# First two projection blocks side by side, state space scalars behind the first mean, second output matrix unsigned on GpSimd

## The chip, the cores and the metric

The kernel runs on one core of one Trainium2 chip. The metric is device time in microseconds (us) of one execution, the median of several runs.

## What is computed

Two layers of a hybrid block on 16 meta tokens and 512 tokens (528 columns), 1024 features. Cut to what the change touches:

```
hn   = rmsnorm(h, norm1_g[l])
proj = hn @ w_in[l]                       # 23 blocks of 128 columns
sq, sk, sv, rq, rk, rv, rg, u = split(proj)
... stick-breaking attention of sq, sk, sv; retention of rq, rk, rv, rg ...
# state space mixer on u, 16 groups of 16 channels, 64 states each
dt = exp(log_dt); mag = exp(lr * dt); ar = mag * cos(li * dt); ai = mag * sin(li * dt)
fr = ((ar - 1) * lr + ai * li) / den;  fi = (ai * lr - (ar - 1) * li) / den
bbr = fr * br - fi * bi;  bbi = fr * bi + fi * br
xr, xi = scan(a, bu)                      # complex linear recurrence
y = xr @ c_re - xi @ c_im                 # the minus sign is what the change moves
y = gelu(y + d * u); so = y * sigmoid(y @ w_glu)
h = h + concat(sb_o, ro, so) @ w_out[l]
h = h + (silu(hn2 @ w_gate[l]) * (hn2 @ w_up[l])) @ w_down[l]
```

## The kernel before, in words

Features lie on the partitions: `h` is eight tiles of 128 x 528. A product of the weights with the features is made in three passes of reduced precision: both operands are split into a high and a low half (`wh` and `wl`, `xh` and `xl`), and `mm3` (line 346) multiplies, for each of the eight feature tiles, high by high, weight high by feature low, and weight low by feature high, each for two halves of 264 columns. One block of 128 output columns is 8 x 3 x 2 = 48 matmuls into two PSUM banks.

A weight block is a `Unit` (line 273): `load` brings it into one of two buffers `wr`, ScalarE casts the high half, and VectorE or GpSimd subtracts it for the low half (the list `WENG` in the plan of line 312 names the engine; the first block has VectorE, the second GpSimd, the third VectorE). `weight()` (line 326) keeps units loading and splitting ahead.

The sum of squares of the first norm is not awaited: the first three blocks (`HOLD`) are multiplied with the unnormed features, `Norm.finish` (line 410) then makes the mean with four matmuls into `nps`, and the evictions on VectorE (`scaled`, line 1073) multiply by its reciprocal root `R`.

At the start `load_h` (line 1027) loads the first feature tile, then the first weight block in four pieces, and the other tiles, with the second weight block behind the fifth tile. `Norm.parts` splits a tile into `xh` (ScalarE) and `xl` (VectorE); the squares follow in a loop of their own (line 1051). Then `first_params` (line 1055) is spawned. It calls `s5_scalars` (line 451), some 70 operations on 16 columns on VectorE, in a chain, and then `s5_params` (line 534).

`s5_params` makes the matrices of the state space mixer of one layer: the input matrices (`ws`, `we`), the output matrices `gg` (line 609, real part `ri` = 0 and imaginary part `ri` = 1, each from two products `gx`), the blocks `bbd` and their products with `gg` into `kps` (line 641), and the phasors. Its argument `engines` is VectorE and GpSimd for the first layer, and GpSimd twice for the second, whose matrices are made during the first layer's feed-forward part. The imaginary output matrix carries a minus sign, so line 629 takes a VectorE instruction with a scalar, whatever `engines` says. `s5_mix` (line 702) waits for these matrices.

The order of the work is written by a planner in the kernel itself: lanes are generators, `spawn` puts one on a list with a due time, and `tick`, called between the matmuls, runs those that are due by a clock of planned engine times (`spend`, line 96). `now[0][1]` is the due time of the lane that runs. Each engine then works through its queue in order; a scheduler of the framework places instructions in the queues by the order of emission and by readiness.

Of the kernel before, what the change touches and what calls it, by code (L numbers as in the profile page):

```python
# [12 lines left out]
ALU = mybir.AluOpType  # L13
# [5 lines left out]
T = NM + S  # L19
# [69 lines left out]
def hybrid_kernel(ctx, tc, A, out, dbg=None):  # L89
# [444 lines left out]
    def s5_params(l, engines, scal, par):  # L534
# [74 lines left out]
        def outputs():  # L609
# [6 lines left out]
            for ri in range(2):  # L616
                mul, add, sub = on(engines[ri])
                pr, pi = powers(0, 5)
                x1, x2 = (gp.tile([P, 640], F32, tag="g", name=nm("gx")) for _ in range(2))
                mul(v4(x1, 5), wide(c_r, 5), pi if ri else pr)  # L620
                mul(v4(x2, 5), wide(c_i, 5), pr if ri else pi)
                yield
                for q in range(2):
                    r = slice(64 * q, 64 * q + 64)
                    for hf in range(2):
                        o = gg[ri, hf][r, :].rearrange("p (m c) -> p m c", c=32)[:, :, 16 * q:16 * q + 16]
                        a, b = (x[r, 320 * hf:320 * hf + 320].rearrange("p (m c) -> p m c", c=16) for x in (x1, x2))
                        if ri:
                            V.scalar_tensor_tensor(out=o, in0=a, scalar=-1.0, in1=b, op0=ALU.mult, op1=ALU.subtract)
                        else:  # L630
                            sub(o, a, b)
                yield
            bbd = [tt("bbd"), tt("bbd")]
            for ri, src in ((0, bbr), (1, bbi)):
                G.memset(bbd[ri][:, :256], 0.0)
                for q in range(2):
                    engines[ri].tensor_copy(
                        out=bbd[ri][64 * q:64 * q + 64, :256].rearrange("p (t c) -> p t c", c=32)[:, :, 16 * q:16 * q + 16],
                        in_=src[64 * q:64 * q + 64])
            yield  # L640
            for hf in range(2):
                yield from banks(1)
# [59 lines left out]
    def s5_mix(l, u, par, ys):  # L702
# [3 lines left out]
        for hf in range(2):  # L706
# [39 lines left out]
            V.tensor_tensor(out=y1, in0=fi, in1=pi, op=ALU.mult)  # L746
            yield
            G.tensor_tensor(out=xr, in0=xr, in1=y1, op=ALU.subtract)
            V.tensor_tensor(out=xi, in0=fr, in1=pi, op=ALU.mult)
            V.tensor_tensor(out=y2, in0=fi, in1=pr, op=ALU.mult)  # L750
            yield
            G.tensor_tensor(out=xi, in0=xi, in1=y2, op=ALU.add)
            yield
            y = tt("ysm")
            for b in range(2):
# [268 lines left out]
        res.append(o)  # L1024


    def load_h(k):
        nc.sync.dma_start(out=h[k], in_=A["h0"][k])
        if k == 0:
            nc.sync.dma_start(out=cols, in_=A["cols"])  # L1030
            u = Unit(*plan[0])
            u.parts = ()
            for i in range(4):
                for _ in u.split(u.load(i, 4)):
                    pass
            units.append(u)
        elif k == 4:
            u = Unit(*plan[1])
            u.load()
            u.parts = u.split()  # L1040
            units.append(u)
            u.use()
            splits[0] = 2

    nrm = Norm(0, 48)
    for k in range(KD):
        load_h(k)
        nrm.parts(k)
    for i in (90, 96):
        G.tensor_scalar(out=cols[:, i:i + 2], in0=cols[:, i:i + 2], scalar1=0.125, scalar2=None, op0=ALU.mult)  # L1050
    for k in range(KD):
        nrm.square(k)
    par = []

    def first_params():
# [3 lines left out]
        yield from s5_params(0, (V, G), scal, par)  # L1059

    scal = []
    spawn(first_params())
    for l in range(LAYERS):
        got = {}
        mix = [None] * 8

        def proj(n, p):
            w = weight()
            ps = open_ps(T)
            mm3(ps, w, nrm.x)  # L1070
            return ps

        def scaled(n, ps):
            t = tt(n)
# [47 lines left out]
        spawn(ret_lane())  # L1122
        held = []
        for i, (n, p) in enumerate(proj_order(l)):
            held.append((n, p, proj(n, p)))
            if i == HOLD[l]:
                nrm.finish()
            if i >= HOLD[l]:
                for n, p, ps in held:
                    spawn(after(n, p, scaled(n, ps)), busy["V"])  # L1130
# [151 lines left out]
```

## Time and profile before

| | |
|---|---|
| median of 3 runs | 1380.3 us (1379.69 to 1380.94) |
| the profiled execution's own time | 1384.1 us |
| its span, first to last instruction | 1382.4 us |
| TensorE (PE) busy | 1352.0 us |
| VectorE (DVE), ScalarE (ACT), GpSimd (POOL) busy | 806.3, 618.1, 514.6 us |
| mean granted clock of TensorE | 0.995 |

The profile comes from one execution. PE is TensorE's matmuls and PEld its weight loads, DVE is VectorE, ACT ScalarE, POOL GpSimd, SPq the queue of SyncE that issues the loads. L121 is a helper through which nearly every instruction goes, so instructions are told apart by the tiles they write and read. A matmul's time in the trace includes its way through the array; how fast they follow one another is read from their starts. Idle time of an engine that is not the bottleneck costs nothing.

### The profile page before, as it was taken

The page shows a single profiled execution, that of the slowest core. Times are in us where ns is not written, and L with a number is a line of the kernel's source. Part 1 is how long each engine was busy: PE and PEld are TensorE (multiplying, and loading weights), DVE is VectorE, ACT ScalarE, POOL GpSimd, SP SyncE. Part 2 cuts the span into 40 slices and gives each one's busy share as a digit, 9 for nine tenths or more (in the row PEclk, how much of TensorE's full clock was granted, in tenths as well). Part 3 has the DMA queues.
Part 4 walks back from the last instruction along what each step waited for, and adds up shares of the span by engine and source line. Part 5 has one row for each costly group of instructions (what it writes and reads, how often), then busy time and mean ns, then how long its engine had stood idle before and what let it go on. Part 6 is the DMA issues. An engine that isn't in the chain of part 4 may idle for free.

```text
span 1382.4 us, 22757 instructions
## 1 busy us (share of the span) xinstructions
PE 1352.0 (98%) x9188; PEld 1241.3 (90%) x9188; DVE 806.3 (58%) x1312; ACT 618.1 (45%) x1002; POOL 514.6 (37%) x624
## 2 busy tenths in 40 slices
PE   6999999999899999999999999999999999999998
PEld 6989999999899999999999998998788888888886
DVE  8874858767456445534567386555585543554453
ACT  5456676555252233312354664874354422332231
POOL 5685648322899112201234534562232210220120
PEclk9999999999999999999999999999999999999999
DMA  4221212323221322322232220123232332233223
GB/s 156 70 74 50 78 46 71 94 77 108 84 78 59 109 92 92 92 92 88 78 110 70 71 93 32 70 59 90 86 105 95 102 93 92 92 96 103 92 79 104
DMA packets 38985, 118.27 MB, mean 86 GB/s; under 512 B 4960, under 2 KB 5472, under 8 KB 38880
## 3 DMA queue, kind: packets, MB, share of 16 engines
q1 hardware_dynamic: 38880, 116.82, 25.9%
q8 instruction: 72, 1.18, 0.3%
q14 instruction: 33, 0.27, 0.1%
HBM read 111.46 MB, written 2.10 MB: 82 GB/s over the span
## 4 chain that ended last, share of the span: by engine, by line
PE 75%; DVE 4%; POOL 3%; issue 1%; ACT 1%; SPq 0%; DMA 0%; DVEq 0%; ACTq 0%
PE pj L133 67%; PE z L133 4%; PE ro L133 1%; PE hps L133 1%; PE av L133 1%; PE yps L133 1%; DVE wl L121 1%; DVE y L121 0%; DVE fr L121 0%; POOL st L121 0%; POOL py L121 0%; PE sc L133 0%; POOL gx L121 0%; POOL bb L121 0%; PE rtp L139 0%
## 5 line engine op out<-in xcount | busy, mean ns | idle before, releaser
L133 PE MATMUL pj<-xh,wh 128*128 128x264 f32 (+1 forms) x1792 | 447.8, 310 | 14.6 <-ACT wh L121 5.3
L133 PE MATMUL pj<-xl,wh 128*128 128x264 f32 (+1 forms) x1792 | 450.5, 311 | 1.6 <-DVE xl L121 1.6
L133 PE MATMUL pj<-xh,wl 128*128 128x264 f32 (+1 forms) x1792 | 447.5, 310 | 1.6 <-DVE wl L121 1.6
L121 ACT CAST wh<-wr 128x1024 fp32r<-128x1024 f32 (+3 forms) x209 | 205.9, 987 | 412.7 <-PE pj L133 378.6
L133 PEld LDWEIGHTS pj<-xh,wh 128*128 128x128 f32 x1792 | 296.8, 190 | 33.1 <-issue 7.4
L133 PEld LDWEIGHTS pj<-xl,wh 128*128 128x128 f32 x1792 | 297.2, 190 | 20.2 <-DVE xl L121 2.4
L133 PEld LDWEIGHTS pj<-xh,wl 128*128 128x128 f32 x1792 | 297.0, 191 | 18.7 <-DVE wl L121 1.8
L121 DVE TENSOR_TENSOR wl<-wr,wh 128x1024 fp32r<-128x1024 f32 (+3 forms) x166 | 249.6, 1505 | 72.4 <-ACT wh L121 72.1
L133 PE MATMUL pj<-hi,wh 128*128 128x264 f32 (+1 forms) x720 | 192.5, 322 | 0.0
L133 PE MATMUL pj<-lo,wh 128*128 128x264 f32 (+1 forms) x720 | 192.4, 321 | 0.0
L133 PE MATMUL pj<-hi,wl 128*128 128x264 f32 (+1 forms) x720 | 191.8, 321 | 0.1
L121 POOL TENSOR_TENSOR up<-ga,up 128x528 f32<-128x528 f32 (+1 forms) x44 | 62.0, 1409 | 344.8 <-DVE up L121 344.7
L121 POOL TENSOR_TENSOR wl<-wr,wh 128x1024 fp32r<-128x1024 f32 (+2 forms) x43 | 96.8, 2252 | 137.3 <-ACT wh L121 117.8
L121 DVE TENSOR_TENSOR h<-h,pj 128x264 f32<-128x264 f32 (+1 forms) x144 | 69.4, 510 | 134.7 <-PE pj L133 134.5
L133 PEld LDWEIGHTS pj<-hi,wl 128*128 128x128 f32 x720 | 119.5, 188 | 11.0 <-DVE wl L121 0.5
L133 PEld LDWEIGHTS pj<-hi,wh 128*128 128x128 f32 x720 | 119.4, 188 | 10.9 <-ACT wh L121 0.6
L133 PEld LDWEIGHTS pj<-lo,wh 128*128 128x128 f32 x720 | 119.4, 188 | 10.5
L121 POOL TENSOR_TENSOR lo<-ga,hi 128x528 fp32r<-128x528 f32 (+1 forms) x44 | 59.0, 1340 | 158.3 <-ACT hi L121 158.2
L121 DVE TENSOR_TENSOR up<-pj,R 128x264 f32<-128x264 f32 (+1 forms) x66 | 32.1, 514 | 95.2 <-PE pj L133 95.2
L121 ACT ACTIVATE si<-si,bias 128x528 f32<-128x528 f32 (+1 forms) x44 | 32.1, 730 | 95.3 <-DVE si L121 95.3
L121 DVE TENSOR_TENSOR ga<-si,up 128x528 f32<-128x528 f32 (+1 forms) x44 | 31.7, 719 | 73.8 <-ACT si L121 58.7
L121 POOL TENSOR_TENSOR lo<-sp,hi 128x432 fp32r<-128x432 f32 (+2 forms) x36 | 46.4, 1301 | 34.4 <-ACT hi L121 34.3
(228 smaller groups left out, 1710.9 us busy)
## 6 DMA issues: line engine op xcount, KB each, us to landing
wr<-in_w_in_dram SPq DMA_DIRECT2D x45, 512.0 KB, 3.4
wr<-in_w_gate_dram SPq DMA_DIRECT2D x44, 512.0 KB, 3.4
wr<-in_w_up_dram SPq DMA_DIRECT2D x44, 512.0 KB, 3.4
wr<-in_w_down_dram SPq DMA_DIRECT2D x32, 512.0 KB, 3.5
wr<-in_w_out_dram SPq DMA_DIRECT2D x16, 384.0 KB, 3.2
wr<-in_w_down_dram SPq DMA_DIRECT2D x16, 384.0 KB, 3.1
rc<-in_rope_dram SPq DMA_DIRECT2D x12, 264.0 KB, 3.7
rs<-in_rope_dram SPq DMA_DIRECT2D x12, 264.0 KB, 3.8
```

What stands on the lines that cost most here:

```text
L121: return f(*a, **k)
L133: nc.tensor.matmul(out, lhsT=lhsT, rhs=rhs, start=start, stop=stop, skip_group_check=more)
```

## The change

The first two blocks are loaded in three pieces each, between the feature tiles, and multiplied tile by tile in turn into four banks. The squares are made between the tiles. `first_params` is spawned after the first mean. The imaginary output matrix loses its sign and is made on the engine that `engines` names; the sign goes into `bbd` and into `xi`. The lane that makes the output matrices gets a due time 2000 ns later before the products with `bbd`.

```diff
--- before.py
+++ after.py
@@ -625,18 +625,16 @@
                     for hf in range(2):
                         o = gg[ri, hf][r, :].rearrange("p (m c) -> p m c", c=32)[:, :, 16 * q:16 * q + 16]
                         a, b = (x[r, 320 * hf:320 * hf + 320].rearrange("p (m c) -> p m c", c=16) for x in (x1, x2))
-                        if ri:
-                            V.scalar_tensor_tensor(out=o, in0=a, scalar=-1.0, in1=b, op0=ALU.mult, op1=ALU.subtract)
-                        else:
-                            sub(o, a, b)
+                        (add if ri else sub)(o, a, b)
                 yield
             bbd = [tt("bbd"), tt("bbd")]
             for ri, src in ((0, bbr), (1, bbi)):
                 G.memset(bbd[ri][:, :256], 0.0)
                 for q in range(2):
-                    engines[ri].tensor_copy(
+                    engines[ri].tensor_scalar(
                         out=bbd[ri][64 * q:64 * q + 64, :256].rearrange("p (t c) -> p t c", c=32)[:, :, 16 * q:16 * q + 16],
-                        in_=src[64 * q:64 * q + 64])
+                        in0=src[64 * q:64 * q + 64], scalar1=-1.0 if ri else 1.0, scalar2=None, op0=ALU.mult)
+            now[0][1] += 2000
             yield
             for hf in range(2):
                 yield from banks(1)
@@ -746,10 +744,10 @@
             V.tensor_tensor(out=y1, in0=fi, in1=pi, op=ALU.mult)
             yield
             G.tensor_tensor(out=xr, in0=xr, in1=y1, op=ALU.subtract)
-            V.tensor_tensor(out=xi, in0=fr, in1=pi, op=ALU.mult)
+            V.scalar_tensor_tensor(out=xi, in0=fr, scalar=-1.0, in1=pi, op0=ALU.mult, op1=ALU.mult)
             V.tensor_tensor(out=y2, in0=fi, in1=pr, op=ALU.mult)
             yield
-            G.tensor_tensor(out=xi, in0=xi, in1=y2, op=ALU.add)
+            G.tensor_tensor(out=xi, in0=xi, in1=y2, op=ALU.subtract)
             yield
             y = tt("ysm")
             for b in range(2):
@@ -1024,32 +1022,33 @@
         res.append(o)
 
 
-    def load_h(k):
+    nrm = Norm(0, 48)
+    units += [Unit(*plan[0]), Unit(*plan[1])]
+    for k in range(KD):
         nc.sync.dma_start(out=h[k], in_=A["h0"][k])
         if k == 0:
             nc.sync.dma_start(out=cols, in_=A["cols"])
-            u = Unit(*plan[0])
-            u.parts = ()
-            for i in range(4):
-                for _ in u.split(u.load(i, 4)):
-                    pass
-            units.append(u)
-        elif k == 4:
-            u = Unit(*plan[1])
-            u.load()
-            u.parts = u.split()
-            units.append(u)
-            u.use()
-            splits[0] = 2
-
-    nrm = Norm(0, 48)
-    for k in range(KD):
-        load_h(k)
-        nrm.parts(k)
+
+        q = []
+        if k < 4:
+            q = [(units[k % 2], k // 2, 4)]
+        elif k < 6:
+            q = [(units[k % 2], 1, 2)]
+        for u, i, pieces in q:
+            c = u.load(i, pieces)
+            nrm.parts(k)
+            for _ in u.split(c):
+                pass
+        if not q:
+            nrm.parts(k)
+        if k:
+            nrm.square(k - 1)
+    nrm.square(KD - 1)
+    for u in units:
+        u.parts = ()
+    splits[0] = 2
     for i in (90, 96):
         G.tensor_scalar(out=cols[:, i:i + 2], in0=cols[:, i:i + 2], scalar1=0.125, scalar2=None, op0=ALU.mult)
-    for k in range(KD):
-        nrm.square(k)
     par = []
 
     def first_params():
@@ -1059,16 +1058,24 @@
         yield from s5_params(0, (V, G), scal, par)
 
     scal = []
-    spawn(first_params())
     for l in range(LAYERS):
         got = {}
         mix = [None] * 8
 
-        def proj(n, p):
-            w = weight()
+        def proj(w):
             ps = open_ps(T)
             mm3(ps, w, nrm.x)
             return ps
+
+        def two_proj():
+
+            ws = [weight(), weight()]
+            pss = [open_ps(T), open_ps(T)]
+            xh, xl = nrm.x
+            for k in range(KD):
+                for ps, w in zip(pss, ws):
+                    mm3(ps, tuple(t[:, k:k + 1, :] for t in w), (xh[k:k + 1], xl[k:k + 1]), first=k == 0, last=k == KD - 1)
+            return pss
 
         def scaled(n, ps):
             t = tt(n)
@@ -1122,9 +1129,16 @@
         spawn(ret_lane())
         held = []
         for i, (n, p) in enumerate(proj_order(l)):
-            held.append((n, p, proj(n, p)))
+            if l == 0 and i < 2:
+                if i == 0:
+                    first = two_proj()
+                held.append((n, p, first[i]))
+            else:
+                held.append((n, p, proj(weight())))
             if i == HOLD[l]:
                 nrm.finish()
+                if l == 0:
+                    spawn(first_params())
             if i >= HOLD[l]:
                 for n, p, ps in held:
                     spawn(after(n, p, scaled(n, ps)), busy["V"])
```

## Rows read from the trace of the kernel before

**Rows 1.** Totals of the page: busy us, share of the span, instructions.
```profile
PE 1352.0 (98%) x9188; PEld 1241.3 (90%) x9188; DVE 806.3 (58%) x1312; ACT 618.1 (45%) x1002; POOL 514.6 (37%) x624
```
**Rows 2.** TensorE's waits over the span: us in total, times, longest.
```profile
PE pj L133 <- DVE xl L121: 1.6, 2, 1.0
PE kps L133 <- POOL bbd L121: 1.5, 1, 1.5
```
**Rows 3.** Timeline, TensorE, 5 to 36 us: start, us, engine, operation, [idle before].
```profile
5.29 0.81 PE L133 MATMUL pj<-xh,wh 128*128 128x264 f32 x2 [5.29 <-ACT wh L121]
...
9.67 0.81 PE L133 MATMUL pj<-xh,wh 128*128 128x264 f32 x2 [2.69 <-ACT xh L121]
...
15.04 0.64 PE L133 MATMUL pj<-xh,wl 128*128 128x264 f32 x2
...
15.48 0.53 PE L133 MATMUL pj<-xh,wh 128*128 128x264 f32 x2
...
25.88 0.41 PE L133 MATMUL pj<-xh,wh 128*128 128x264 f32 x2
...
26.12 0.40 PE L133 MATMUL pj<-xl,wh 128*128 128x264 f32 x2
...
29.63 0.51 PE L133 MATMUL pj<-xh,wl 128*128 128x264 f32 x2 [1.63 <-DVE wl L121]
...
35.10 0.28 PE L133 MATMUL nps<-hi,meanw 128*128 128x264 f32 x1
```
**Rows 4.** Timeline, the other engines, 1 to 16 us.
```profile
1.71 1.85 SPq L284 DMA_DIRECT2D wr<-in_w_in_dram  x4
...
13.29 2.39 POOL L121 TENSOR_TENSOR wl<-wr,wh 128x1024 fp32r<-128x1024 f32 x1 [1.65 <-ACT wh L121]
13.47 2.25 DVE L121 TENSOR_TENSOR s5w<-s5w 128x16 f32<-128x16 f32 x1
```
**Rows 5.** Tile `s5w`, 0 to 45 us: ns min/median/max, first and last start.
```profile
L121 DVE TENSOR_TENSOR s5w<-s5w x19: 161/175/2245, 13.5 to 36.9; 128x16 f32<-128x16 f32 x19
...
L121 DVE TENSOR_TENSOR s5w<-cols,s5w x2: 165/166/168, 5.2 to 5.3; 128x16 f32<-128x16 f32 x2
```
**Rows 6.** Windows: us, busy (instructions) PE, PEld, DVE, ACT, POOL, PEclk, DMA.
```profile
10.00:15.00 5.00, 5.00 (x22) 4.70 (x22) 4.97 (x13) 4.49 (x7) 2.62 (x3) 1.00 0.83 329
...
0.00:35.00 35.00, 23.76 (x144) 22.51 (x145) 28.39 (x96) 17.38 (x28) 19.83 (x44) 0.95 0.45 154
...
60.00:100.00 40.00, 36.58 (x252) 33.73 (x251) 33.73 (x116) 19.30 (x36) 34.35 (x94) 0.91 0.19 67
370.00:375.00 5.00, 2.02 (x13) 2.05 (x14) 4.97 (x9) 0.69 (x2) 5.00 (x10) 0.91 0.00 0
375.00:380.00 5.00, 5.00 (x34) 5.00 (x33) 1.45 (x3) 1.38 (x2) 4.84 (x6) 0.75 0.31 105
```
**Rows 7.** Timeline, 365 to 373 us, GpSimd, VectorE and TensorE.
```profile
366.76 2.64 POOL L121 TENSOR_TENSOR gx<-braw,s5p 128x640 f32<-128x640 f32 x2
...
369.44 2.94 DVE L121 SCALAR_TENSOR_TENSOR gg<-gx,gx 64x320 f32<-64x320 f32 x4 [3.97 <-POOL gx L121]
...
372.98 0.36 PE L133 MATMUL pj<-xh,wh 128*128 128x264 f32 x1 [3.77 <-DVE ga L121]
```
**Rows 8.** Groups, VectorE, 40 to 100 us: busy, mean ns | idle before, releaser.
```profile
L121 DVE TENSOR_TENSOR gx<-braw,s5p 128x640 f32<-128x640 f32 x2 | 3.3, 1682 | 3.9 <-DMA braw<-in_bc_dram 3.9
```
**Rows 9.** Tile `gg`, 0 to 500 us: ns min/median/max, first and last start.
```profile
L121 DVE SCALAR_TENSOR_TENSOR gg<-gx,gx x8: 484/608/1381, 62.5 to 371.9; 64x320 f32<-64x320 f32 x8
...
L121 POOL TENSOR_TENSOR gg<-gx,gx x4: 868/874/879, 360.4 to 363.0; 64x320 f32<-64x320 f32 x4
```
**Rows 10.** Tile `uc`, 0 to 300 us: the state space lane's first instructions.
```profile
L121 ACT COPY uc<-u x16: 418/430/438, 115.5 to 185.9; 32x132 f32<-32x132 f32 x16
```
**Rows 11.** Timeline, VectorE, 276 to 291 us, around the first output projection.
```profile
281.05 0.71 DVE L121 TENSOR_TENSOR lo<-glu,hi 128x528 fp32r<-128x528 f32 x1 [0.29 <-ACT hi L121]
...
289.10 0.76 DVE L121 TENSOR_TENSOR h<-h,pj 128x264 f32<-128x264 f32 x2
```

## The prediction

> **What bounds the kernel now.** I first read the page's totals: TensorE is busy for 1352.0 us, 98% of the span [rows 1]. A change can gain only in the 30 us in which TensorE waits and where its clock is low; work of another engine counts only if a TensorE wait ends with it. So the second view was TensorE's waits, summed by what released them [rows 2]: 1.6 us on the low halves `xl` of the features and 1.5 us on `bbd` are among them; the larger ones stand with their place in the timeline, which came third.
>
> *The start* [rows 3]. TensorE starts at 5.29 us, waits 2.69 us for the second feature tile and later 1.63 us for a low weight half `wl`; the mean of the first norm follows the third block at 35.10 us. Three blocks are 3 x 48 = 144 matmuls. Late in the stretch a pair starts after 0.24 us (25.88, 26.12), 0.12 us each: 17.3 us of work, so 12.5 of these 29.8 us are lost. Part is rate: from 15.04 to 15.48 a pair takes 0.44 us, 0.22 us each, the lower of the two clock levels (1.2 against 2.4 GHz). So it runs from 9.67 on, right after the wait, until about 15.5. The windows view gives a granted clock of 1.00 there [rows 6]; I go by the spacing.
>
> *Why low halves are late.* VectorE's queue holds the scalars of the state space model between the splits, from 5.2 to 37.1 us [rows 5]. They are 16 columns wide with a median of 0.175 us, but the one at 13.47 took 2.25 us, beside GpSimd's weight split of 13.29 to 15.68 [rows 4].
>
> *60 to 100 us.* VectorE (33.7 of 40 us) and GpSimd (34.4) are nearly full, TensorE is busy for 36.6 us and the granted clock is 0.91 [rows 6]: 3.4 us idle, and 40 x 0.09 x 2 = 7.2 us at the lower level, which cost 7.2 x (1 - 0.12 / 0.22) = 3.3 us.
>
> *365 to 380 us*, the first layer's feed-forward part [rows 7]. VectorE's `gg` instruction stands at the head of its queue for 3.97 us until GpSimd has made `gx`; behind it stand the evictions `ga`, which free TensorE's banks. TensorE waits 3.77 us, and then the granted clock is 0.91 and 0.75 in two windows of 5 us [rows 6]: 5 x 0.34 x 2 = 3.4 us at the lower level, 1.5 us lost.
>
> **The change part by part.**
>
> *Two blocks side by side.* Each feature tile gets 12 matmuls instead of 6. The bytes stay; SP issues one load more, at 1.85 / 4 = 0.46 us [rows 4], and the second block's quarters pass ahead of later tiles, so the last tile may land half a microsecond later, when TensorE has a backlog that covers it. SP's load of the third weight waits until the first weight is split and its buffer free, some 4 us later than now; two blocks of 48 x 0.12 = 5.8 us each cover it. In the first 35 us ScalarE is busy for 17.4 us and GpSimd for 19.8 [rows 6]: the same work fits into 29. GpSimd splits the second block's weight in three pieces instead of one of 2.39 us.
> I count the losses that remain: 1.5 us waiting for the second block's first quarter (not shown before; nothing at best, 2.7 us at worst, the wait for a tile that it replaces; I take the middle, as a quarter is half a tile in size); 1.0 us in the first six matmuls (0.6 of rate, 0.4 on their low half); the lower clock for 6 us from about 8 us, as long as before, 27 matmuls x 0.10 = 2.7 us; 1.0 us on low halves. That is 6.2 instead of 12.5: **gain 6** (bounds 3, if both kinds of wait stay, and 9).
>
> *The scalars behind the mean.* They leave VectorE's first stretch (counted above) and come back after the third block, behind that block's evictions. Lines 451 to 532 issue 70 of them: from below 70 x 0.175 = 12 us, from above the 32 us that they take now among the splits. Queued behind them are the evictions of blocks 4 and 5 and the products of the state space matrices. The latter wait for a load that VectorE today awaits for 3.9 us [rows 8], so the first few microseconds are free. But the stretch of 60 to 100 us gets fuller. Its bounds are a gain of 3.4 us (its waits vanish) and a loss of 6.7 (what it costs now, once more); I take **a loss of 1.5**, nearer the row as it stands, since four `gg` instructions (4 x 0.61 us, rows 9) leave VectorE there too.
> The state space lane then starts later. Today it begins at 115.5 us, as its matrices get ready [rows 10], and its last split ends at 281.76, while the output projection that uses it cannot start before the previous part's last pair of evictions at 289.10 [rows 11]: 7.3 us of slack, of which TensorE's 6 us of lead eat most. If the matrices are L later in absolute time, TensorE stands still for L - 1.3 us. I take L = 3, **a loss of 1.7** (bounds 0 and 10).
>
> *The second output matrix on GpSimd.* Four adds at 0.87 us, measured on GpSimd for the same shape [rows 9], 3.5 us a layer, take the place of four VectorE instructions. In layer 2's matrices, made during the first feed-forward part, no VectorE instruction waits for `gx` any more: 3.77 + 1.5 = 5.3 us. GpSimd is full there (5.00 of 5 us, rows 6), so its products for the feed-forward part queue 3.5 us longer, but TensorE needs those only in the down projection; I take off 0.3: **gain 5** (bounds 0 and 5.3). The sign goes into `xi`, where four instructions of VectorE take another form, and into `bbd`, where a multiplication takes the place of a copy: nothing, as TensorE waits nowhere for `xi` (its wait for `bbd` is priced next); without that cover some tenths of a microsecond.
>
> *2000 ns more before the blocks' products.* TensorE waits 1.5 us for `bbd` [rows 2]. The planner now emits these matmuls 2 us later; GpSimd's four adds lie before `bbd`, but the planner prices them itself. **Gain 1.2** (bounds 0 and 1.5).
>
> Sum: 6 + 5 + 1.2 - 1.5 - 1.7 = 9.0 us. The profiled execution took 1384.1 us, so 1375.1; it lies 3.8 us above the median of the runs, 1380.3, which gives 1371.3, rounded **1371 us**.
>
> **A rule against it.** At 13.47 a 0.17 us instruction of VectorE lasted as long as GpSimd's split beside it [rows 4]. The Trainium skill, page "SBUF — State Buffer", section "Who interferes with whom", says that a VectorE instruction with two SBUF inputs and a GpSimd instruction that reads SBUF exclude one another, whichever came first holding the port to its end. The trace agrees (2.25 us against 0.17). By that rule GpSimd's new adds cost VectorE about their own length, which is the third rival. The Trainium skill, page "Perfetto Trace Analysis", section "Optimizing Scalar/DVE Operations", warns likewise that moving work between these two might not help.
>
> **The rivals.**
> 1. *VectorE's crowding takes it back.* The scalars, stretched by GpSimd's instructions, meet evictions at 60 to 100 us, and the 6.7 us lost there double: 5.2 more than I took, 1376. For it: both engines are full there. Against: VectorE idles for 3.9 us just before [rows 8]. Chance 0.18.
> 2. *The state space lane becomes the bound: slower.* Place: the second part of the first output projection. If the scalars take 32 us again, they end at 61 instead of 37 and L is 24; TensorE waits 22.7 us instead of 1.7, 21 more than I took: 1392. It decides from about L = 12 on, where it eats all the gain. Against: VectorE has no splits of feature tiles left between the scalars. Chance 0.08.
> 3. *The port.* GpSimd's adds hold up VectorE's evictions in the feed-forward part for 3.5 us, and TensorE with them: 1374.5. For it: the 2.25 us row. Against: behind an add that lasts 0.87 us there is only a short hold-up, and a block gives TensorE 5.8 us of work. Chance 0.12.
> 4. *More than that.* Nothing lost at 60 to 100 and in the lane, and the start gains 9: 1371.3 - 3 - 3.2, 1365. Chance 0.10.
>
> **How the numbers follow.** My case (1366 to 1376) has 0.52. About 0.2%, 2.8 us, is what a measurement of this kernel can tell from no change: below 1377.5 is faster. Half of rival 1's spread and nearly all of rival 3's lie there, with my case and rival 4: 0.82 faster. The other half of rival 1 and a rest of 3 give 0.10, rival 2 gives 0.08. The range 1364 to 1379 takes in rivals 1, 3 and 4 and leaves out rival 2 and the tails.
>
> **What would show it.** Right, if the first `nps` matmul comes at about 29 us; if no scalar of the state space model stands on VectorE before it; if the wait for `ga` and the lower clock near 370 us are gone, and the wait for `bbd`. Wrong, if TensorE waits at the first output projection's second part, if 60 to 100 us loses far more than 6.7 us, or if the wait near 370 us comes back under another name.

## The result, and the profile after

The changed kernel takes 1392.65 us (median of 4 runs, 1390.1 to 1393.14), the kernel before 1380.62 us beside it: a ratio of 1.0081, 95% interval 1.0066 to 1.0096. It is slower by 12 us, where 9 us of gain were forecast; the range of the prediction ended at 1379. The profiled execution has a span of 1390.7 us, against 1382.4 before. Of all runs below one was slow, 2274.75 us at a mean granted clock of 0.636 (the changed kernel with the early call), and that kernel's figure is the median of its three fast runs.

**Totals.** The page's first part of the kernel after; it answers to [rows 1]:

```profile
PE 1354.9 (97%) x9188; PEld 1245.7 (90%) x9188; DVE 804.5 (58%) x1303; ACT 617.5 (44%) x1003; POOL 512.4 (37%) x634
```

TensorE is busy for 2.9 us more with the same 9188 matmuls, and stands idle for 35.8 us instead of 30.4. VectorE has nine instructions fewer and GpSimd ten more.

**By stretch.** Windows of the kernel after (us, busy time and instructions of PE, PEld, DVE, ACT, POOL, then PEclk, DMA share, GB/s), and under them the same windows of the kernel before from 100 us on:

```profile
0.00:35.00 35.00, 25.85 (x172) 24.98 (x173) 29.76 (x93) 19.60 (x33) 21.61 (x47) 0.95 0.50 169
60.00:100.00 40.00, 35.20 (x274) 33.99 (x273) 31.10 (x99) 19.37 (x34) 32.93 (x85) 1.00 0.17 57
100.00:200.00 100.00, 96.58 (x692) 90.57 (x692) 60.53 (x105) 59.24 (x120) 62.64 (x69) 0.95 0.21 67
200.00:300.00 100.00, 92.94 (x738) 87.58 (x736) 78.88 (x153) 52.06 (x98) 35.95 (x30) 0.97 0.21 63
300.00:400.00 100.00, 94.89 (x769) 93.09 (x769) 59.74 (x90) 43.58 (x63) 52.20 (x51) 0.98 0.29 95
```

```profile
100.00:200.00 100.00, 100.00 (x762) 93.03 (x761) 61.78 (x122) 68.14 (x134) 56.09 (x49) 1.00 0.18 57
200.00:300.00 100.00, 98.70 (x797) 93.95 (x797) 74.91 (x144) 55.85 (x105) 50.80 (x38) 1.00 0.26 78
300.00:400.00 100.00, 96.23 (x781) 96.05 (x780) 61.48 (x92) 44.31 (x63) 57.19 (x77) 0.98 0.28 96
```

Up to 100 us the change gains. The first 35 us hold 172 matmuls instead of 144 [rows 6], and from 60 to 100 us the granted clock is 1.00 where it was 0.91. The loss lies from 100 to 400 us, where little of the change itself stands: TensorE is busy for 284.4 us of these 300 instead of 294.9, and the clock column gives 100 x (0.05 + 0.03 + 0.02) x 2 = 20 us at the lower level instead of 4. A microsecond at the lower level loses 1 - 0.24 / 0.44 = 0.45 us of work, by the pairs of matmuls in [rows 3], so that is 10.5 + 16 x 0.45 = 17.7 us lost. The hundredths of the clock column make this good to a few microseconds.

**Waits.** TensorE's waits over the span of the kernel after, the largest nine; they answer to [rows 2]:

```profile
PE pj L133 <- ACT wh L121: 5.7, 1, 5.7
PE wps L139 <- POOL ws L121: 5.1, 2, 2.7
PE sc L133 <- DVE sc L121: 4.5, 3, 2.8
PE av L133 <- DVE rq L121: 3.4, 1, 3.4
PE pj L133 <- DVE u L121: 3.0, 1, 3.0
PE hps L133 <- ACT hsq L121: 2.6, 3, 1.3
PE pj L133 <- DVE wl L121: 2.2, 1, 2.2
PE pj L133 <- DVE sq L121: 1.8, 1, 1.8
PE ro L133 <- DVE sc L121: 1.5, 1, 1.5
```

The waits for `xl`, for `bbd` and for `ga` are no longer among the large ones. In their place stand `ws` (the input matrices of the second layer), `sc` (retention), `rq` and `u`. By their place in the timeline, the waits of over 1 us between 100 and 400 us are `av` for `rq` at 179.9 us, retention's products `sc` and `ro` at 220.7, 265.9 and 268.5 us (5.7 us together), `hps` at 251.7 us, and `ws` at 394.6 and 398.6 us; `u` and `sq` lie at 77.6 and 83.0 us. At the second part of the first output projection, whose evictions run from 302.3 to 316.8 us, TensorE does not wait, as these windows of the kernel after show:

```profile
290.00:310.00 20.00, 20.00 (x165) 18.30 (x164) 12.25 (x31) 9.92 (x21) 5.49 (x8) 1.00 0.20 55
310.00:330.00 20.00, 20.00 (x167) 20.00 (x166) 17.38 (x34) 11.29 (x17) 6.64 (x4) 1.00 0.38 119
```

**The start.** Timeline of TensorE (it answers to [rows 3]), then the tile `s5w` over the span ([rows 5]), both of the kernel after:

```profile
10.68 0.64 PE L133 MATMUL pj<-xh,wh 128*128 128x264 f32 x2
11.12 0.44 PE L133 MATMUL pj<-xh,wl 128*128 128x264 f32 x2
11.40 0.41 PE L133 MATMUL pj<-xh,wh 128*128 128x264 f32 x2
11.64 0.41 PE L133 MATMUL pj<-xl,wh 128*128 128x264 f32 x2
...
30.06 0.28 PE L133 MATMUL nps<-hi,meanw 128*128 128x264 f32 x1
```

```profile
L121 DVE TENSOR_TENSOR s5w<-s5w x19: 159/166/1327, 9.9 to 38.5; 128x16 f32<-128x16 f32 x19
...
L121 DVE TENSOR_TENSOR s5w<-cols,s5w x2: 168/168/168, 5.2 to 5.3; 128x16 f32<-128x16 f32 x2
```

TensorE no longer waits for the second tile; pairs are 0.44 us apart until 11.12 and 0.24 from 11.40 on, where the change came at about 15.5 before. The first `nps` comes at 30.06 us, 5.0 us earlier. But the scalars stand where they stood: from 5.2 us on, the last one at 38.5 (36.9 before), although the call that issues them now comes behind the third block. Their inputs are ready from the start, and the framework's scheduler places instructions by readiness as well as by the order of emission. Moving the call did not move them.

**The lane.** What did move is the lane behind the scalars. Tile `ws` from 50 to 120 us, first of the kernel before, then of the kernel after (ns min/median/max, first and last start):

```profile
L139 PE MATMUL wps<-ident,ws x16: 272/273/300, 70.1 to 77.2; 128*128 128x128 f32 x16
...
L121 POOL TENSOR_TENSOR ws<-btmp,btmp x4: 922/952/1083, 60.2 to 63.1; 64x256 f32<-64x256 f32 x4
```

```profile
L139 PE MATMUL wps<-ident,ws x16: 270/272/273, 95.4 to 101.1; 128*128 128x128 f32 x16
...
L121 POOL TENSOR_TENSOR ws<-btmp,btmp x4: 733/738/1620, 62.0 to 65.1; 64x256 f32<-64x256 f32 x4
```

The data are 2 us later (65.1 against 63.1), the transposes that read them 25 us later. TensorE waited for nothing there: the transposes stand later in its queue, so the planner placed them later. The state space lane starts at 136.8 us (its first `uc` copy on ScalarE) instead of 115.5 [rows 10].

**Layer 2's matrices.** Timeline of GpSimd and of TensorE and a window, kernel after; they answer to [rows 7] and [rows 6]:

```profile
391.86 7.37 POOL L121 TENSOR_TENSOR ws<-btmp,btmp 64x256 f32<-64x256 f32 x8
...
394.59 1.34 PE L139 MATMUL wps<-ident,ws 128*128 128x128 f32 x8 [2.42 <-POOL ws L121]
...
398.60 1.12 PE L139 MATMUL wps<-ident,ws 128*128 128x128 f32 x4 [2.66 <-POOL ws L121]
```

```profile
396.00:402.00 6.00, 3.40 (x16) 3.41 (x17) 1.24 (x2) 0.93 (x2) 5.78 (x6) 0.57 0.25 87
```

VectorE's wait for `gx` and TensorE's 3.77 us for `ga` are gone. GpSimd, full as before, gives the lost time back 20 us later: TensorE waits 2.42 and 2.66 us for `ws`, and the granted clock is 0.57 behind it.

### The profile page after: what moved, and what is told of

It reads as the page before. It is cut to its first block, busy times and chain, and to the rows that moved or that the text cites. A ratio compares the mean times of both kernels' runs of the same rounds, so it can differ in the third digit from the quotient of the medians.

```text
span 1390.7 us, 22774 instructions
## 1 busy us (share of the span) xinstructions
PE 1354.9 (97%) x9188; PEld 1245.7 (90%) x9188; DVE 804.5 (58%) x1303; ACT 617.5 (44%) x1003; POOL 512.4 (37%) x634
## 4 chain that ended last, share of the span: by engine, by line
PE 84%; DVE 9%; POOL 3%; ACT 1%; issue 1%; DMA 1%; SPq 0%; DVEq 0%
PE pj L133 72%; PE z L133 5%; PE hps L133 1%; PE ro L133 1%; PE av L133 1%; DVE fr L121 1%; DVE s5w L121 1%; DVE ysm L121 1%; DVE fi L121 1%; DVE st L121 1%; DVE y L121 1%; DVE wl L121 1%; POOL ws L121 1%; PE kps L133 1%; POOL gg L121 1%
## 5 line engine op out<-in xcount | busy, mean ns | idle before, releaser
L121 POOL TENSOR_TENSOR up<-ga,up 128x528 f32<-128x528 f32 (+1 forms) x44 | 60.8, 1381 | 344.1 <-DVE up L121 344.1
L121 POOL TENSOR_TENSOR wl<-wr,wh 128x1024 fp32r<-128x1024 f32 (+3 forms) x45 | 97.1, 2158 | 117.5 <-ACT wh L121 107.4
L133 PEld LDWEIGHTS pj<-lo,wh 128*128 128x128 f32 x720 | 119.9, 189 | 10.4
```

Of the source, the lines that this page charges most:

```text
L121: return f(*a, **k)
L133: nc.tensor.matmul(out, lhsT=lhsT, rhs=rhs, start=start, stop=stop, skip_group_check=more)
```

## The experiments

All figures stand against the kernel before on the same chip (medians of 1379.6 to 1381 us). The column "lane starts" is the state space lane's first `uc` copy on ScalarE, "first `ro`" the start of the first retention pair's output products on TensorE, "last split" the end of the split of the state space lane's result, which the output projection's second part needs. These three columns come from one profiled execution of each kernel, which lies up to 8 us from its median.

| kernel | median us | ratio, 95% | lane starts | first `ro` | last split |
|---|---|---|---|---|---|
| before | 1380.6 | | 115.5 | 184.6 | 281.8 |
| after | 1392.65 | 1.0081 (1.0066 to 1.0096) | 136.8 | 223.4 | 298.3 |
| two blocks only | 1377.4 | 0.9979 (0.9970 to 0.9988) | 114.9 | 186.7 | 290.3 |
| late call only | 1399.5 | 1.0139 (1.0117 to 1.0161) | 137.7 | 225.7 | 309.5 |
| unsigned only | 1387.7 | 1.0052 (1.0032 to 1.0072) | 129.3 | 210.5 | 289.9 |
| unsigned, layer 2 | 1380.45 | 1.0003 (0.9993 to 1.0012) | 115.6 | 185.7 | 284.6 |
| unsigned, layer 1 | 1388.3 | 1.0065 (1.0052 to 1.0079) | 129.2 | 210.4 | 290.5 |
| due 1 us later | 1390.6 | 1.0073 (1.0060 to 1.0086) | 125.3 | 244.2 | 296.5 |
| due 2 us earlier | 1399.0 | 1.0129 (1.0108 to 1.0149) | 122.1 | 245.6 | 300.3 |
| one bank kept | 1392.8 | 1.0086 (1.0062 to 1.0109) | 119.9 | 233.6 | 287.0 |

### The parts, one at a time

**The changed kernel with the early call.**

```diff
+    spawn(first_params())
...
-                if l == 0:
-                    spawn(first_params())
```

> The changed kernel with the state space scalars spawned ahead of the projections again, as before; two blocks side by side, unsigned output matrix and the later due time stay. Lane theory (the scalars' new place starts the state space lane 21 us late, and its VectorE work then meets GpSimd's splits at 170 to 270 us, where TensorE lost some 17 us to waits and the lower clock): the lane begins near 115 us again, those losses fall below 4 us, the time is 1374 to 1380. GpSimd theory (the loss comes from the adds that moved to GpSimd): 1388 or more, as in the changed kernel. Start theory (splits of the second block side by side leave the kernel's order worse): also 1388 or more.

1387.9 us, ratio 1.0055 (1.0033 to 1.0077): the early call gives back only 4.7 us. Something else in the change costs as well.

**The late call alone**, in the kernel before:

```diff
-    spawn(first_params())
...
+                if l == 0:
+                    spawn(first_params())
```

> The kernel before with one edit: the scalars are spawned behind the first mean. Lane theory: the lane begins 15 to 25 us later than 115 us, TensorE waits between 170 and 300 us, the time is 1386 to 1395. GpSimd theory: no adds moved, so the time is 1375 to 1383, and the splits of the features are earlier. Start theory: 1375 to 1383 as well.

1399.5 us: 19 us lost by moving one call, with the scalars on VectorE from 5.3 to 36.8 us as before. The transposes of `ws` come at 102.1 us, and its `ws` was ready 33 us earlier (last start 68.2).

**The two blocks side by side alone** (the diff's hunks from line 1024 on, without the move of the call):

> The kernel before with only the first two blocks side by side; scalars early, the signed output matrix on VectorE. Lane theory: the first mean comes 2 to 5 us earlier (33 to 30 us), the lane begins at 110 to 117 us, the time is 1374 to 1379. Start theory: slower than before, 1385 or more. GpSimd theory: 1374 to 1379, like the lane theory.

1377.4 us: faster than both kernels, by 2.9 us against before. The first `nps` comes at 30.1 us as in the kernel after, so 5.0 us of lead become 2.9 at the end.

**The unsigned matrix alone, then layer by layer:**

```diff
-                            V.scalar_tensor_tensor(out=o, in0=a, scalar=-1.0, in1=b, op0=ALU.mult, op1=ALU.subtract)
+                            (engines[1] if l == 1 else V).tensor_tensor(out=o, in0=a, in1=b, op=ALU.add)
...
```

This is the edit for layer 2 alone; layer 1 alone has `l == 0`, and the run with both takes the line of the diff. In all three the signs go into `bbd` and `xi` of both layers, as in the diff.

> The kernel before with only the unsigned output matrix on GpSimd (signs in the blocks and in xi), without the later due time. Lane theory: the 3.8 us wait for the evictions near 370 us goes; GpSimd's queue is 3.5 us longer and the transposes of the input matrices wait for it instead, as in the changed kernel (5 us there), so 1378 to 1383. GpSimd theory: 1386 or more, with the loss in the first layer.

> The kernel before with the unsigned output matrix, made on GpSimd for the second layer's matrices alone; the first layer's stays on VectorE (an add there). Lane theory: the first layer runs as before (the lane begins at 113 to 118 us, the first output projection ends at 322 to 326 us); in the feed-forward part the wait for ga (3.8 us) is replaced by the transposes' waits for GpSimd's ws (some 5 us) with the lower clock behind them, so 1379 to 1383. If the adds in the first layer cost nothing and the feed-forward part alone made the loss of the unsigned matrix, this run would show 1386 to 1389.

> The kernel before with the unsigned output matrix, made on GpSimd for the first layer's matrices alone. Lane theory: the state space lane begins near 129 us as in the run with both, the state space and retention lanes end at 288 to 292 and 309 to 314 us instead of 281.8 and 302.7, TensorE waits at the first output projection, and the time is 1383 to 1388, nearly all of the loss of the unsigned matrix. If the loss sat in the feed-forward part, it would be 1379 to 1382.

Both layers 1387.7 us, layer 2 alone 1380.45, layer 1 alone 1388.3 (1.0065, 1.0052 to 1.0079). So layer 2's part, for which 5 us were forecast, is worth nothing, and layer 1's, priced at nothing, costs 8 to 9. The new signs are in the run with layer 2 alone too, so they are not what costs. TensorE's largest waits with layer 2's part alone:

```profile
PE pj L133 <- ACT wh L121: 5.1, 1, 5.1
PE wps L139 <- POOL ws L121: 4.7, 2, 2.4
PE pj L133 <- DVE wl L121: 4.3, 1, 4.3
```

The wait for `ga` has left the list, 4.7 us for `ws` have come; from 360 to 420 us TensorE is busy for 55.3 us at a clock of 0.94 against 54.8 at 0.97.

The prices of the parts do not add up. Alone they come to 19.1 + 7.3 - 2.9 = 23.5 us of loss; together they make 12.

**Two tries to keep layer 2's gain** beside the two blocks: VectorE's `gg` instructions 6 us later and the products 2 us later, and GpSimd's version with transposes and products 12 us later.

```diff
+                if ri and l:
+                    now[0][1] += 6000
...
```

> Two blocks side by side, scalars early, signed matrix on VectorE; but for the second layer's matrices the lane that makes the output matrices is due 6 us later before VectorE's signed subtraction, and 2 us later before the products with bbd. Lane theory: first layer as in the run with two blocks only (1377.4); the wait for ga near 370 us (3.7 us and 1.5 us of lower clock) and the wait for bbd (1.4 us) go, so 1370 to 1374. If GpSimd's full queue is the bound there and the wait only moves (to ws, as with the adds on GpSimd), 1376 to 1379.

> Two blocks side by side and scalars early as in the run with two blocks only; the unsigned output matrix on GpSimd for the second layer's matrices alone; and for those the transposes of the input matrices and the products with bbd are due 12 us later. Queue theory of the feed-forward part (TensorE meets whatever GpSimd's full queue makes late, and only a later place in TensorE's own order helps): the waits for ga, for ws and for bbd between 360 and 430 us all go, so 1370 to 1374. If another product of GpSimd's queue becomes late instead (up, lo), TensorE waits there and the time is 1376 to 1380.

1379.96 us (1.0006, 0.9996 to 1.0015) and 1380.9 us (0.9998, 0.9986 to 1.0010): both lose the 2.9 us of the two blocks. In the first the wait for `ga` stays at 3.8 us, so, as with the scalars, the due time did not decide the place on VectorE; in the second it is 1.5 us, without profit.

### First theory: a late lane is the price

**The lane held back** by 14 us with its matrices unmoved, and **the matrices 16 us later** with the call unmoved:

```diff
+            if l == 0:
+                now[0][1] = max(now[0][1], busy["PE"]) + 14000
+                yield
```

> The kernel before with nothing moved; the first layer's state space lane is only held back by 14 us in the planner once its matrices are ready. Lane theory: lateness alone is enough; the lane begins at 128 to 132 us, retention and state space end 7 us or more later, TensorE waits before or in the first output projection, and the time is 1384 to 1392. If the loss came from crowded engines (scalars beside evictions, adds on GpSimd) and not from the lane's start, this run would be within 2 us of before, 1379 to 1383.

```diff
         scal.extend(s5_scalars())
+        now[0][1] += 16000
```

> The kernel before, scalars in their place, but the lane that makes the first layer's matrices is due 16 us later in the planner after the scalars. Planner theory (moving the scalars' call did not move them on VectorE, where they start at 5.2 us in every run; it gave the matrices a later due time, and with it TensorE's transposes and products a later place in its order): the transposes come at 90 to 105 us instead of 70, the lane begins at 128 to 140 us, and the time is 1388 to 1400. If the scalars' place itself cost the time, this run is within 3 us of before.

1393.2 us (1.0097, 1.0081 to 1.0112) and 1394.5 us (1.0088, 1.0060 to 1.0116). Lateness as a price would give about this: 13 and 14 us, for 14 and 16. But the runs don't say whether lateness itself is paid for. Lanes ask for PSUM banks with `banks(n)` out of a budget of five (`BANKS`), and wait until n are free at once; a lane that comes later finds others holding them.

**A sixth bank** (`BANKS = 6`), in the kernel after and in the kernel before:

> The changed kernel with the lanes' budget of PSUM banks raised from 5 to 6. Bank theory (a late state space lane is dear because it competes with stick-breaking and retention for the five banks): retention's first pair ends before 235 us instead of 252, its third before 308 instead of 316, and the time falls to 1378 to 1386. If the lateness costs through the planner's order alone, whatever the banks: 1389 to 1395.

> The kernel before with the lanes' budget raised from 5 to 6, the control of the run with six banks. Bank theory: its lanes are not late, so little changes, 1376 to 1384. If six banks take TensorE's own double buffers away, 1385 or more.

1415.6 us (1.0243, 1.0219 to 1.0267) and 1404.5 us (1.0165, 1.0141 to 1.0189): 23 us worse in either. The budget leaves the other banks of the eight to the projections' own double buffering, so this run mixes two things and decides nothing on the order.

### Second theory: the order in which the lanes get the banks

**The due time 1 us later**, nothing else:

```diff
         scal.extend(s5_scalars())
+        now[0][1] += 1000
```

> Edit: the kernel before, with the due time of the lane of the state space matrices 1 us later, behind the scalars, which stay where they are. The race for the banks of the planner's budget: the second input matrix asks for its bank a moment after the attention lanes have taken the free ones, so its transposes on TensorE come 20 us or more later (they start by 76.1 us before), the lane starts at 121 us or later (115.5 before), and the time is at least 4 us above that of the kernel before, 1385 to 1392 us. Lateness of the due time alone: 1 us of due time is worth 1 us or less (16 us of it cost 14 us), nothing moves by more than 2 us, and the time is within 1.5 us of the kernel before.

1390.6 us: one microsecond of due time costs 10. Tile `ws`, 50 to 120 us:

```profile
L139 PE MATMUL wps<-ident,ws x16: 270/272/330, 71.8 to 111.8; 128*128 128x128 f32 x16
...
L121 POOL TENSOR_TENSOR ws<-btmp,btmp x4: 777/869/1196, 57.4 to 62.2; 64x256 f32<-64x256 f32 x4
```

The last transposes go from 77.2 to 111.8 us, 49 us after the last of their data. Lateness as a price of its own cannot do that.

**The late call with the old due time:**

```diff
         scal.extend(s5_scalars())
+        now[0][1] = busy["PE"] + 2700
```

> Edit: the kernel before with the call moved behind the first mean, and the due time of the lane set back to about what it was before the move. Lateness of the due time: the transposes of the input matrices are back at 70 to 77 us, the lane starts at 116 to 118 us, and the time is 1381 to 1383 us. The race for the banks: the order of the requests has changed as well, so the transposes stay at 85 us or later, the lane starts at 125 us or later, and the time is 1388 us or more.

1396.4 us (1.0116, 1.0103 to 1.0130), transposes at 105.2 us, lane at 140.1. Setting the due time back does not bring the lane back.

**The due time 2 us earlier:**

```diff
         scal.extend(s5_scalars())
+        now[0][1] -= 2000
```

> Edit: the kernel before, with the due time of the lane of the state space matrices 2 us earlier, nothing else. If lateness of this lane is the price by itself, an earlier one costs nothing: the lane starts at 111 to 115 us (115.5 before) and the time is 1378 to 1381.5 us. If the order in which the lanes get the banks of the budget decides, an earlier request takes a bank from another lane: the lane starts at 111 to 114 us, but the third retention pair is done at 310 us or later (302.7 before), and the time is 1384 us or more.

1399.0 us: asking earlier costs 19 us. The lane did not come earlier, against what was expected (122.1 us), but its first products did not suffer (`es` at 135.3 us, 134.2 before); retention did, whose third pair is done at 332.0 us instead of 302.7.

**One bank kept for the matrices**, with the late call, with layer 1's unsigned matrix, and in the kernel before:

```diff
-        if free[what] < n:
-            yield lambda: free[what] >= n
+        if free[what] < n + kept[what]:
+            yield lambda: free[what] >= n + kept[what]
...
```

The lines left out let the first layer's matrices take the last bank: the transposes of `ws` in all three runs, and in the last two the products with `bbd` as well.

> Edit: the call moved behind the first mean, and one bank of the planner's budget kept for the transposes of the first layer's input matrices until they are done. The race for the banks: the transposes come back from 102 and 107 us to 70 to 82 us, the lane starts some 3 to 15 us earlier than at 137.7, and the time falls from 1399.5 us by 5 us or more. Lateness of the due time or crowding on VectorE: the transposes come by at most 5 us earlier, and the time stays within 3 us of 1399.5.

> Edit: the unsigned matrix on GpSimd in the first layer alone, and one bank of the budget kept for the transposes and the products with bbd of the first layer. The race for the banks: the products with bbd come back from 108.4 and 122.8 us to about 100 and 113, the lane starts at 116 to 121 us instead of 129.2, and the time falls from 1388.3 to 1380 to 1384 us. GpSimd's own load: the products stay at 106 us or later, the lane at 126 us or later, and the time stays at 1386 to 1390 us. A kept bank costs the other lanes something either way, up to some microseconds.

> Edit: the kernel before, with one bank of the budget kept for the transposes and the products with bbd of the first layer's matrices until they are done; scalars, signs and start as before. It is the control for the run that keeps a bank beside the unsigned matrix in the first layer (1391.7 us). If the kept bank costs the other lanes, the lane starts at 113 to 117 us and the time is 1386 us or more, by the retention pairs. If it costs nothing, the time is 1380 to 1382 us, and the loss in the other run is the unsigned matrix's own.

With the late call the transposes come back from 102.1 to 82.9 us and the time falls to 1393.3 (1.0096, 1.0079 to 1.0112), 6 us less; the lane gains only 1 us. With layer 1's unsigned matrix the products are back at 96.1 us and the lane at 118.4, yet the first `ro` is at 226.2 and the time 1391.7 us (1.0081, 1.0066 to 1.0096): the forecast of 1380 to 1384 fails. The control tells why: a kept bank alone, in the kernel before, costs 12 to 13 us. Its lane starts at 119.9 us and its last split is at 287.0 us, earlier than in the kernel with the two blocks (290.3), which is the fastest of all. So in the control the state space lane is not what is paid for. VectorE's timeline there shows what the output projection waits for:

```profile
300.57 0.77 DVE L121 TENSOR_TENSOR h<-h,pj 128x264 f32<-128x264 f32 x2
...
314.53 0.71 DVE L121 TENSOR_TENSOR lo<-o,hi 128x528 fp32r<-128x528 f32 x1 [0.70 <-ACT hi L121]
317.98 1.11 DVE L121 TENSOR_TENSOR h<-h,pj 128x264 f32<-128x264 f32 x3 [2.74 <-PE pj L133]
```

The third part's first eviction comes 17 us after the second part's last pair, behind the split of retention's third pair (314.53); in the kernel before it was 2 us. In other runs it is the state space lane after all. With the due time 1 us later, and with layer 1's unsigned matrix alone, in this order, TensorE waits before the second part for the lane's result (`hi<-glu`):

```profile
292.04 0.51 PE L133 MATMUL pj<-hi,wh 128*128 128x264 f32 x2 [3.13 <-ACT hi L121]
```

```profile
289.85 1.69 PE L133 MATMUL pj<-hi,wh 128*128 128x264 f32 x6 [3.68 <-ACT hi L121]
```

The first retention pair is late in both kinds of run (first `ro` in the table). Tile `sc`, 140 to 290 us, of the kernel before, of the one with a kept bank, and of the kernel after:

```profile
L133 PE MATMUL sc<-rm,rm x60: 172/272/373, 178.9 to 288.6; 64*128 64x128 f32 x48, 64*16 64x16 f32 x12
...
L133 PE MATMUL ro<-sc,rv x40: 204/272/324, 184.6 to 262.1; 128*64 128x128 f32 x32, 16*64 16x16 f32 x8
```

```profile
L133 PE MATMUL sc<-rm,rm x40: 173/272/373, 228.8 to 278.7; 64*128 64x128 f32 x32, 64*16 64x16 f32 x8
...
L133 PE MATMUL ro<-sc,rv x40: 204/273/323, 233.6 to 282.9; 128*64 128x128 f32 x32, 16*64 16x16 f32 x8
```

```profile
L133 PE MATMUL sc<-rm,rm x40: 172/272/373, 215.9 to 265.9; 64*128 64x128 f32 x32, 64*16 64x16 f32 x8
...
L133 PE MATMUL ro<-sc,rv x40: 204/304/476, 223.4 to 273.7; 128*64 128x128 f32 x32, 16*64 16x16 f32 x8
```

The first pair's scores (`sc`) start at 178.9, 228.8 and 215.9 us. They come in the program behind the running sums `st`, where the lane asks for three banks at once. Tile `kv` (140 to 250 us) gives the last of these sums, in the same order:

```profile
L121 DVE TENSOR_TENSOR st<-st,kv x6: 203/219/225, 168.9 to 170.6; 64x64 f32<-64x64 f32 x6
```

```profile
L121 DVE TENSOR_TENSOR st<-st,kv x6: 211/220/227, 200.8 to 202.9; 64x64 f32<-64x64 f32 x6
```

```profile
L121 DVE TENSOR_TENSOR st<-st,kv x6: 213/219/227, 189.9 to 191.2; 64x64 f32<-64x64 f32 x6
```

From the last sum to the first score it is 8.3 us before, 25.9 with a kept bank and 24.7 in the kernel after. The scores read `q` and `k`, not the sums, so no data are late; the lane stood in the planner. The stage ahead is late too: the pair's `rv` is evicted at 150.8 us before and at 147.8 after, and the transposes that read it start at 153.5 and 168.6. But there the lane also waits for the pair's `rk`, whose rotation on GpSimd starts at 145.7 us before and at 164.0 after, so that this gap is not a wait for banks of its own.

The start of the first `ro` separates all twenty kernels. The five in which the first `ro` starts by 188 us (before, two blocks only, unsigned in layer 2, and the two tries at layer 2) take 1377.4 to 1380.9 us. The fifteen in which it starts at 208.6 us or later take 1387.7 us or more. The last split of the state space lane separates nothing: 290.3 to 291.5 us stands beside 1377.4 to 1380.9, 287.0 beside 1392.8. Its start does separate them, 114.9 to 116.2 us against 118.4 and later, so the separation alone does not tell retention from the lane. What speaks against lateness as a price is the size: a lane 2.9 us late (layer 1's unsigned matrix with a kept bank) goes with 11 us, one 4.4 us late (the control) with 12 to 13, and one 21.3 us late (the changed kernel) with 12.

**What is shown, and what stays open.** Shown: one or two microseconds in when the matrices ask, or one bank less for the others, shifts the first retention pair by 49 to 61 us and costs 10 to 19 us. Shown too: the work that TensorE then waits for differs: retention's products in the changed kernel (beside `av`) and in the control, the state space lane's result with 1 us of due time. That it is the wait for three banks at once that holds retention up is argued from the program's text and these gaps; the trace has no record of the planner's waits. The late call and layer 1's adds on GpSimd each delay the first retention pair, and either alone is enough. Retention was not held back, or put first, by itself, so its share in the price is not measured. Why the costs without a sixth bank lie between 7 and 19 us stays open, and a sixth bank with the projections' share left alone was not tried.

## Why the prediction was wrong

- **The start: right, mis-sized.** Forecast 6, first `nps` at about 29 us; it comes at 30.1, 5.0 us earlier. Alone it leaves 2.9 us at the end. The term that was too small is "1.0 us on low halves": TensorE waits 2.2 us for `wl` until 16.94 us, with state space scalars still ahead of that split on VectorE, and pairs are 0.44 us apart again from 19.00 to 21.20 us. Nor did the slow rate begin with the wait at 9.67 us: in the kernel before, too, matmuls are 0.22 us apart from 5.68 us on.
- **"They leave VectorE's first stretch": failed.** A call further down in the program was taken for a later place in VectorE's queue. The scalars ran from 5.2 to 38.5 us, and the loss put down for them at 60 to 100 us did not come; that stretch got a little better: 4.8 us idle at a clock of 1.00, against 3.4 us idle and 7.2 us at the lower level. For the whole move of the call the sum has 1.5 + 1.7 = 3.2 us; alone it costs 19.
- **"I take L = 3" and "TensorE stands still for L - 1.3 us": the step that failed.** L was 21.3 us. The formula would make that 20 us at the output projection, at whose second part TensorE did not stand still. The step treats the lane as a chain by itself with slack at its end, while lanes share TensorE's queue and five banks: 2 us in the data became 25 us at the transposes. TensorE waited elsewhere instead: 5.7 us at retention's `sc` and `ro`, which the prediction does not mention, and 3.4 us at `av`, with the lower clock behind them. Between 100 and 340 us these waits, 1.1 us at `hps` and that clock make up the loss; that the order of the requests for banks brought them about is argued, as said above.
- **The unsigned matrix, "gain 5": failed twice.** Of layer 2's wait it asked what goes, and named the down projection as next; `ws`, made by the same full GpSimd, was next (5.1 us and a clock of 0.57). Layer 1's four adds, costed at nothing, cost 8 to 9 us: the products with `bbd` go from 99.8 to 108.4 us. With a kept bank they are back at 96.1, so GpSimd's own load is not what made them late.
- **2000 ns:** the wait for `bbd` is gone; its 1.2 us can't be told in the time.
- **The second rival gave the time, 1392 with a chance of 0.08, and not the cause; that the two agree is luck.** Its condition, scalars that take 32 us again behind the mean, never came true, and at its place, the second part of the output projection, the changed kernel has no wait.
- **The first rival fell** with 60 to 100 us. The third did not show either: from 276 to 392 us TensorE is busy throughout. The fourth fell with the start, which gained 5 and not 9.

## What to carry to other kernels

Where a planner interleaves lanes under a shared budget, a part cannot be priced by its own chain: a request that comes one microsecond later, or earlier, can change who gets the resource, and with it the lane that is waited for at the end. Before moving a call, ask what it moves in each engine's queue (here nothing on VectorE) and what in the order of requests, and run the smallest shift alone as a probe. When an engine is full, removing one wait for it only names the next thing it makes late.

## What was not expected of the hardware

A wait on TensorE in the kernel after begins with two engines that share nothing in the program. The scans of this tile over the span, the timeline of VectorE, GpSimd and TensorE, and a window behind it:

```profile
L121 DVE TENSOR_TENSOR_SCAN fi<-rho,fi x16: 396/404/2502, 170.9 to 846.6; 128x132 f32<-128x132 f32 x16
```

```profile
175.07 3.71 DVE L121 TENSOR_TENSOR_SCAN fi<-rho,fi 128x132 f32<-128x132 f32 x2
...
176.02 2.46 POOL L121 TENSOR_TENSOR wl<-wr,wh 128x1024 fp32r<-128x1024 f32 x1
...
179.43 0.77 DVE L121 TENSOR_TENSOR rq<-pj,R 128x264 f32<-128x264 f32 x2
...
179.91 0.58 PE L133 MATMUL av<-hi,v 128*128 128x256 f32 x1 [3.42 <-DVE rq L121]
```

```profile
178.00:189.00 11.00, 9.09 (x43) 9.06 (x44) 7.14 (x11) 4.24 (x9) 7.48 (x7) 0.53 0.30 98
```

Two scans, 0.40 us each by their median, take 3.71 us beside GpSimd's split of 2.46; the eviction `rq` behind them comes late, TensorE waits 3.42 us, and the granted clock is 0.53 from 178 to 189 us. The Trainium skill, page "SBUF — State Buffer", section "Who interferes with whom", says that a VectorE instruction with two SBUF inputs contends with a GpSimd instruction that reads SBUF. A scan has two such inputs, `rho` and `fi`, and this trace agrees (3.71 us where two medians make 0.81). At the rates of [rows 3] that window loses up to 11 x 0.47 x 2 x 0.45 = 4.7 us, more than the wait itself.
